# Experts of a routed MLP in seven groups of one, two or four, and conditioning sums by a ones column and two small DMAs

## The chip, the core and the metric

The kernel runs on one core of a Trainium2 chip. The metric is the device time of one launch in microseconds. The kernel before takes 1269.88 us, the median of three runs (1268.04 to 1272.34).

The engines are named as the profile names them: PE is TensorE (PEld its weight loads), DVE is VectorE, ACT is ScalarE, POOL is GpSimd, SP is SyncE. SP issues the weight loads here, POOL's queue the small transfers. PEclk is the granted clock of PE as a part of its full 2.4 GHz.

## The reference, cut to what matters

256 tokens of width 1024 pass through a first block with two layers and a second block with one. Each layer is modulated by a vector that comes from a condition `c`; the second block ends in 16 experts, of which each token uses two.

```python
def ada_modulation(c, w, b):                 # first block, 4 times; w is 1024 x 3072
    mod = jax.nn.silu(c) @ w + b
    shift, scale, gate = jnp.split(mod, 3, axis=-1)
    ...
h = x * (1.0 + scale) + shift
y = windowed_gqa(h, ...)                     # or recurrent_block(h, ...)
x = layer_norm(DN_ALPHA * x + (1.0 + gate) * y, ln_g[i, 0], ln_b[i, 0])
... the same again with sq_relu_mlp in the place of the mixer
mod_x = ada_modulation_2(cond_x, ada_w, ada_b)   # second block; w is 1024 x 6144
mod_c = ada_modulation_2(cond_c, ada_w, ada_b)

def moe_ffn(h, router_w, router_b, w_gate, w_up, w_down):
    probs = jax.nn.softmax(h @ router_w, axis=-1)
    ...  # best group of four experts by probs + router_b, then the two best experts in it
    for e in range(N_EXPERTS):               # 16 experts, 1024 -> 512 -> 1024
        he = (jax.nn.silu(h @ w_gate[e]) * (h @ w_up[e])) @ w_down[e]
        out = out + combine[:, e:e + 1] * he
```

Everything is in float32.

## The kernel before, in words

**Weights stream in.** A class `Stream` (`W`) holds one list of 1 MB weight loads in the order in which they are used. SP issues them (L193) into a ring of staging buffers `stg`: 5 of them, and for the experts 6 more, so that a load waits until PE has finished with the one 11 places before it. For dense layers ACT makes the high part `wh` of each weight (L218) and DVE the low part `wl` (L223), and each product is three matmuls (`mm3`, L380 to L382). Matmuls of the experts use the float32 weights directly.

**Conditioning runs as filler.** Weights of `ada_w` are spread among the items of the dense layers; `step` (from L229) takes one item at a time. Two ways are used. `ada_fill` multiplies on PE, four column groups of 32 at once (L424), and DVE copies the sums out as rows, `adaR` (L431). `ada_fill_v` accumulates on DVE (`adav`, L455 and L457), which leaves one partial sum on each partition. What is needed for shift and scale is 8 values on each of 128 partitions. Before, PE turns either form into that: `to_cols` (L500) by 16 matmuls for each row of `adaR`, with an identity's columns as the moving side, `sum_cols` (L472) by 8 matmuls for each vector with a column of ones. DVE then reads `gen`, the result in PSUM, and forms `sst` and `ab`, or `ss2`, from it (L559 to L567, L592 to L599). There are five such places: two layers of the first block by `to_cols`, one by `sum_cols`, and in the second block two rows by `to_cols` and one vector by `sum_cols`.

**After each dense layer** `post` runs `residual`: DVE multiplies by the gate, adds, and normalizes (`rr`, L865 to L867 and on), and PE waits for the normalized activations.

**The experts** (`moe_pass`). The router sorts the 14 experts behind the first two by their count of tokens; `RANK` says which place each gets. A selection matrix of ones and zeros (`Sg`) gathers the tokens of one window of 128 slots: `gather` makes the gathered activations by matmuls, `slots` the weights of each slot, `up` gate and up projections (L2406, activations stationary, 512 columns of the expert's weights moving) and the gated product, `turn` transposes it, `down` projects back (L2441), `scatter` adds the slots to their tokens (L2456, L2457). There are eight windows of two experts. In six of them each expert has 64 slots and its own half of PE's columns. In the two `SHARED` ones (1 and 3) two experts share the 128 slots, so each expert's weights pass over all 128 columns, as two separate units. The units are ten. Gate, up and down come as two loads each, so the 16 experts take 96 loads. The first two experts are fixed; the loads of the others wait until the routing is known. If the greatest count exceeds the slots, the whole runs again for the slots behind (`tc.If(over > CAP * base)`, up to three times).

Of the kernel before, what the change touches and what calls it, by code (L numbers as in the profile page):

```python
# [11 lines left out]
F32 = mybir.dt.float32  # L12
# [28 lines left out]
def _consts():  # L41
# [9 lines left out]
    small["slot"] = np.stack([p + 1 + CAP * i for i in range(4)], 1).astype(f)  # L51
# [83 lines left out]
class Stream:  # L135


    def __init__(self, tc, stage, parts, depth, ahead):
# [9 lines left out]
        self.more, self.since = None, 0  # L148

# [79 lines left out]
    def step(self, ahead=None):  # L229

        ahead = self.ahead if ahead is None else ahead
        i = self.pos
# [15 lines left out]
        return it[0], self.hl.pop(i)  # L248

# [21 lines left out]
def tile_model(ctx: ExitStack, tc: tile.TileContext, A, out):  # L271
# [6 lines left out]
    sml = ctx.enter_context(tc.tile_pool(name="sml", bufs=2))  # L278

# [270 lines left out]
    def ada1(i, j):  # L550
# [4 lines left out]
        def fin_ss(R, v=False):  # L555
            ab = cst.tile([128, 2, 8], F32, name=f"ab{idx}")
            tmp = sml.tile([128, 2, 8], F32, name="sst")
            pv = sum_cols(R, 2) if v else to_cols(R, 0)
            V.tensor_add(tmp[:, 0], pv[:, :, 0], adb[:, idx, 0])  # L559
            V.scalar_tensor_tensor(tmp[:, 1], pv[:, :, 1], 1.0, adb[:, idx, 1], op0=OP.add, op1=OP.add)  # L560
            if idx == 0:
                V.tensor_copy(ab[:, 0], tmp[:, 1])
                V.tensor_copy(ab[:, 1], tmp[:, 0])
            else:
# [3 lines left out]
            MOD[i, j] = ab  # L568
# [16 lines left out]
    def ada2(third):  # L585
# [3 lines left out]
        def fin(R):  # L589
            for row in range(2):  # L590
                pv = to_cols(R, row)
# [150 lines left out]
    def moe_items(add):  # L742
# [26 lines left out]
        for w in range(NWIN):  # L769
            for m in ((2 * w,), (2 * w + 1,)) if w in SHARED else ((2 * w, 2 * w + 1),):  # L770
                ups(m)
                if late is not None:
                    downs(late)
                    late = None
# [1519 lines left out]
    def moe_pass(base, W, weigh=None):  # L2294
# [166 lines left out]
        for u, (w, m) in enumerate(units):  # L2461
# [6 lines left out]
            if u:  # L2468
                turn(u - 1, mi())
# [92 lines left out]
```

## Time and profile before

| | us |
|---|---|
| median of three runs | 1269.88 |
| the profiled execution, its own time | 1271.62 |
| its span in the profile | 1269.8 |
| PE busy | 1209.9 (95%) |
| DVE busy | 779.3 (61%) |
| ACT busy | 557.8 (44%) |
| POOL busy | 96.3 (8%) |
| experts, first to last matmul of L2406 and L2441 | 988.4 to 1252.8 |

A busy share over the span is an average over stages. What bounds a stage is read in that stage: from the order of instructions on PE and the gaps between them, from the granted clock, and from which queue waits for which.

### The profile page before, as it was taken

Reading aid. Unit: us, or ns where it says so; the run is one execution under the profiler, and the core shown is the slowest. Engines: PE = TensorE matmul, PEld = TensorE weight load, DVE = VectorE, ACT = ScalarE, POOL = GpSimd, SP = SyncE. Lnnn points to the kernel's source line nnn. Section 1 sums busy time; section 2 is a strip of 40 time slices with the busy share of each in tenths; the row PEclk is TensorE's granted clock in tenths of the full one; section 3 lists DMA queues with packets and bytes.
Section 4 is the critical chain, followed back from the end, with each engine's and each line's share of the span. In section 5 each row is a group of like instructions: output and inputs, shape, how many; then the busy total and the mean of one; then the engine's idle time right before and its main releaser. Section 6 shows DMA issues by size and latency. Waiting matters only on the chain. (4 is left out here: it accounts for less than half of the span.)

```text
span 1269.8 us, 17771 instructions
## 1 busy us (share of the span) xinstructions
PE 1209.9 (95%) x6830; PEld 894.7 (70%) x6830; DVE 779.3 (61%) x1458; ACT 557.8 (44%) x944; POOL 96.3 (8%) x165
## 2 busy tenths in 40 slices
PE   5999799999989999979999999899998999999995
PEld 3757698999866668558989989899996444444432
DVE  3587879767575777685878759868898301110113
ACT  2455454534368766652455536634666111110111
POOL 6000360000013400010000000100000000000000
PEclk9999899989989999988999989999999899999997
DMA  9978498858684562487778846753338779889991
GB/s 291 343 306 301 167 324 318 302 198 305 192 250 123 178 200 69 165 292 253 268 257 288 297 135 201 231 168 117 127 106 324 282 289 413 327 346 375 409 412 53
DMA packets 146693, 317.52 MB, mean 250 GB/s; under 512 B 8120, under 2 KB 97368, under 8 KB 133288
## 3 DMA queue, kind: packets, MB, share of 16 engines
q1 hardware_dynamic: 139768, 304.17, 67.8%
q0 software_dynamic: 6832, 12.13, 3.1%
q8 instruction: 56, 0.92, 0.3%
q14 instruction: 37, 0.30, 0.1%
HBM read 315.23 MB, written 1.05 MB: 249 GB/s over the span
## 5 line engine op out<-in xcount | busy, mean ns | idle before, releaser
L218 ACT ACTIVATE wh<-stg 128x1024 fp32r<-128x1024 f32 x236 | 241.5, 1041 | 245.0 <-issue 98.1
L223 DVE TENSOR_TENSOR wl<-stg,wh 128x1024 fp32r<-128x1024 f32 x233 | 277.7, 1207 | 95.2 <-ACT wh L218 94.1
L380 PE MATMUL gen<-hH,wh 128*128 128x256 f32 x704 | 205.7, 292 | 3.7 <-ACT hH L841 2.6
L382 PE MATMUL gen<-hH,wl 128*128 128x256 f32 x704 | 203.8, 290 | 0.9 <-DVE wl L223 0.9
L381 PE MATMUL gen<-hL,wh 128*128 128x256 f32 x704 | 203.5, 290 | 0.5 <-DVE hL L845 0.5
L380 PEld LDWEIGHTS gen<-hH,wh 128*128 128x128 f32 x704 | 140.1, 199 | 10.4 <-ACT hH L841 4.6
L382 PEld LDWEIGHTS gen<-hH,wl 128*128 128x128 f32 x704 | 139.6, 199 | 2.4 <-DVE wl L223 2.3
L381 PEld LDWEIGHTS gen<-hL,wh 128*128 128x128 f32 x704 | 139.7, 199 | 2.0 <-POOL hL L845 0.7
L380 PE MATMUL acc<-wh,mH 128*128 128x512 f32 x256 | 102.0, 400 | 0.0
L381 PE MATMUL acc<-wl,mH 128*128 128x512 f32 x256 | 100.9, 394 | 0.0
L382 PE MATMUL acc<-wh,mL 128*128 128x512 f32 x256 | 100.7, 394 | 0.0
L2406 PE MATMUL mgu<-stg,wh 128*64 128x512 f32 (+1 forms) x256 | 83.7, 625 | 0.0
L457 DVE SCALAR_TENSOR_TENSOR adav<-stg,csil,adav 128x1024 f32<-128x1024 f32 (+2 forms) x56 | 79.2, 1415 | 6.7 <-DMA stg<-in_ada_w_dram 6.0
L2406 PE MATMUL mgu<-stg,wl 128*64 128x512 f32 (+1 forms) x256 | 78.5, 593 | 0.0
L2441 PE MATMUL mmi<-stg,mhT 128*64 128x512 f32 (+1 forms) x256 | 73.5, 595 | 0.0
L2412 DVE SCALAR_TENSOR_TENSOR mhid<-mgu,mws,mhid 128x512 f32<-128x512 f32 x10 | 7.5, 751 | 86.9 <-PE mgu L2406 86.9
L1492 PE MATMUL gen<-xr,bd 128*128 128x256 f32 (+1 forms) x224 | 59.6, 410 | 0.8 <-DVE xr L1468 0.8
L2441 PEld LDWEIGHTS mmi<-stg,mhT 128*64 128x64 f32 (+1 forms) x256 | 27.7, 150 | 42.3 <-issue 41.4
L2406 PEld LDWEIGHTS mgu<-stg,wl 128*64 128x64 f32 (+1 forms) x256 | 27.4, 150 | 42.7 <-issue 42.0
L2446 ACT ACTIVATE wh<-mmi 128x512 fp32r<-128x512 f32 x16 | 9.6, 597 | 108.5 <-PE mmi L2441 108.5
L380 PEld LDWEIGHTS acc<-wh,mH 128*128 128x128 f32 x256 | 48.8, 191 | 11.5 <-ACT wh L218 1.3
L382 PEld LDWEIGHTS acc<-wh,mL 128*128 128x128 f32 x256 | 48.6, 190 | 11.2 <-issue 0.8
(607 smaller groups left out, 2222.6 us busy)
## 6 DMA issues: line engine op xcount, KB each, us to landing
stg<-in_ada_w_dram SPq DMA_DIRECT2D x72, 1024.0 KB, 5.7
stg<-in_mlp_w_dram SPq DMA_DIRECT2D x64, 1024.0 KB, 5.8
stg<-in_moe_w_up_dram SPq DMA_DIRECT2D x32, 1024.0 KB, 8.6
stg<-in_moe_w_gate_dram SPq DMA_DIRECT2D x32, 1024.0 KB, 8.2
stg<-in_moe_w_down_dram SPq DMA_DIRECT2D x32, 1024.0 KB, 10.8
stg<-in_w_in_dram SPq DMA_DIRECT2D x20, 1024.0 KB, 5.4
stg<-in_rnn_w_in_dram SPq DMA_DIRECT2D x12, 1024.0 KB, 6.3
stg<-in_attn_w_in_dram SPq DMA_DIRECT2D x8, 768.0 KB, 9.2
```

The costliest lines, as they stand in the source:

```text
L218: nc.scalar.activation(h, t[:, sl], AF.Copy)
L223: sub()
L380: PE.matmul(o, ah, bh, start=first, stop=False)
L381: PE.matmul(o, ah, bl, start=False, stop=False)
L382: return PE.matmul(o, al, bh, start=False, stop=last)
L457: V.scalar_tensor_tensor(acc, tv[:, j, :], col[:, k:k + 1], acc, op0=OP.mult, op1=OP.add)
L1492: PE.matmul(pv[c0:c1, q, :], BD[g % 2][:, q, d, o:o + c1 - c0], xr[g][:, kt, :], start=(i == 0), stop=True, skip_group_check=True)
L2406: PE.matmul(ps[sl], gx[c][:, k, o + sl.start:o + sl.stop], t[:, 512 * k:512 * k + 512], start=first, stop=last)
L2412: V.scalar_tensor_tensor(hid, got[1], WS[w][:, j:j + 1], hid, op0=OP.mult, op1=OP.mult)
L2441: PE.matmul(ps[h][sl], hT[:, 2 * c + k, sl], t[:, 1024 * k + 512 * h:1024 * k + 512 * h + 512], start=begin and k == 0, stop=end and k == 1)
L2446: SC.activation(yH[:, h, :], ps[h], AF.Copy)
```

## The change

**Conditioning.** `to_cols` and `sum_cols` are gone. For the DVE form a new `sum_rows` multiplies with a column of ones that is broadcast over 32 columns, which leaves the sums as rows, two or four matmuls of 512 columns; ACT copies them to `adaR`. For both forms a new `row_cols` moves rows to columns by two DMAs on POOL's queue: the rows of `adaR` to a DRAM tile `flat`, and `flat` to `adaC`, 128 partitions of 8 or 16 values. The second waits for the first. The instructions of DVE that use `adaC` are put off by two steps of the stream (`LAG`, `wait_less`), or to the start of the next `post`, if that comes first.

**Experts.** The eight windows become seven, with 2, 1, 4, 2, 1, 2 and 4 experts of 128, 64 or 32 slots each, every expert on column groups of its own. There is no shared window, the units are seven, and the gathers are four groups instead of five. `RANK` puts the experts by their counts into these places. The loads of gate and up, and of down, go by half first and by expert second. The greatest count times the number of experts in its window decides whether a second pass runs.

```diff
-NWIN = 8
-SHARED = (1, 3)
-GROUPS = [(0,), (1, 2), (3, 4), (5, 6), (7,)]
-RANK = [0, 13, 2, 11, 1, 12, 3, 10, 4, 9, 5, 8, 6, 7]
+NUMBERS = [2, 1, 4, 2, 1, 2, 4]
+FIRST = [sum(NUMBERS[:w]) for w in range(len(NUMBERS) + 1)]
+NWIN = len(NUMBERS)
+GROUPS = [(0,), (1, 2), (3, 4), (5, 6)]
+RANK = [0, 6, 7, 8, 9, 2, 3, 1, 4, 5, 10, 11, 12, 13]
+LAG = 2
...
     def step(self, ahead=None):
         ahead = self.ahead if ahead is None else ahead
+        self.wait_less()
...
+    def wait_less(self, all=False):
+        for d in list(self.due):
+            d[0] -= 1
+            if all or d[0] < 0:
+                self.due.remove(d)
+                d[1]()
...
-    def sum_cols(acc, n):
-        ps = gen()
-        pv = ps[:, 0:8 * n].rearrange("p (k s) -> p k s", k=8)
-        for s in range(n):
-            for k in range(8):
-                PE.matmul(pv[:, k, s:s + 1], acc[:, 1024 * s + k:1024 * s + 1024:8], one, start=True, stop=True)
-        return pv
+    def sum_rows(acc, n):
+        ps = gen()
+        for g in range(2 * n):
+            PE.matmul(ps[32 * g:32 * g + 32, :], one.to_broadcast([128, 32]), acc[:, 512 * g:512 * g + 512],
+                      start=True, stop=True)
+        R = sml.tile([128, 512], F32, name="adaR", bufs=1)
+        SC.activation(R[:64 * n, :], ps[:64 * n, :], AF.Copy)
+        return R
+
+    def row_cols(R, row, n, use):
+        C = sml.tile([128, 2, 8], F32, name="adaC", bufs=3)
+        flat = rows.tile([2 * n, 512], F32, name="flat")
+        GP.dma_start(flat, R[row:64 * n:32, :])
+        GP.dma_start(C[:, :n, :], flat.rearrange("(s r) (p k) -> s (r p) k", s=n, k=8).rearrange("s p k -> p s k"))
+        W.due.append([LAG, lambda: use(C)])
...
-    def to_cols(R, row):
-        ps = gen()
-        pv = ps[:, 0:16].rearrange("p (k s) -> p k s", k=8)
-        for r in range(2):
-            for k in range(8):
-                PE.matmul(pv[64 * r:64 * r + 64, k, :], R[:, k::8], ident[:, 32 * r + row::64], start=True, stop=True)
-        return pv
...
-            pv = sum_cols(R, 2) if v else to_cols(R, 0)
-            V.tensor_add(tmp[:, 0], pv[:, :, 0], adb[:, idx, 0])
...
+            row_cols(sum_rows(R, 2) if v else R, 0, 2, use)
...
     def post(y, i, j, nxt):
+        W.wait_less(True)
...
-        def downs(w):
-            m = (2 * w, 2 * w + 1)
-            for i, h in ([(i, h) for i in m for h in range(2)] if w in SHARED else [(i, h) for h in range(2) for i in m]):
-                add(("moe_w_down_2", i, h), partial(down, i, h))
+        def downs(m):
+            for h in range(2):
+                for i in m:
+                    add(("moe_w_down_2", i, h), partial(down, i, h))
...
+        def lanes(w):
+            c = CAP // NUMBERS[w]
+            return [(FIRST[w] + n, slice(c * n, c * n + c)) for n in range(NUMBERS[w])]
...
-                        for j, t in enumerate(ts):
-                            sl = slice(0, 128) if len(m) == 1 else half[j]
+                        for (_, sl), t in zip(m, ts):
                             PE.matmul(ps[sl], gx[c][:, k, o + sl.start:o + sl.stop], t[:, 512 * k:512 * k + 512],
                                       start=first, stop=last)
```

What the change does to the order of instructions is shown at three places. The first is DVE around the first of the five conditioning results, in the attention layer: `den` and `sc` belong to its softmax, `wl` is the low part of a weight, `adav` the next vector's accumulation, `gate` the next gate. Before:

```order
L431 COPY adaR<-adaps 128x512
L1166 TENSOR_SCALAR sc<-sc,den 128x256 x4
L223 TENSOR_TENSOR wl<-stg,wh 128x1024
L457 SCALAR_TENSOR_TENSOR adav<-stg,csil,adav 128x1024
L559 TENSOR_TENSOR sst<-gen,adb 128x8
L560 SCALAR_TENSOR_TENSOR sst<-gen,adb 128x8
```

And DVE at the same place after:

```order
L442 COPY adaR<-adaps 128x512
L1176 TENSOR_SCALAR sc<-sc,den 128x256 x4
L224 TENSOR_TENSOR wl<-stg,wh 128x1024
L468 SCALAR_TENSOR_TENSOR adav<-stg,csil,adav 128x1024 x2
L224 TENSOR_TENSOR wl<-stg,wh 128x1024
L571 TENSOR_TENSOR sst<-adaC,adb 128x8
```

The first use stands behind one more accumulation and one more `wl`, and reads what a DMA brought instead of PSUM.

The second is DVE at the last of the five, in the second block's condition, at the start of `post`. Before:

```order
L485 SCALAR_TENSOR_TENSOR gate<-gen,gate 128x512
L599 TENSOR_TENSOR ss_132<-gen,adb_127 128x8
L865 TENSOR_TENSOR rr<-acc,gate 128x512
L866 TENSOR_TENSOR rr<-xnat,rr 128x512
L867 BN_STATS bst<-rr 128x6
L865 TENSOR_TENSOR rr<-acc,gate 128x512
```

After:

```order
L505 SCALAR_TENSOR_TENSOR gate<-gen,gate 128x512
L875 TENSOR_TENSOR rr<-acc,gate 128x512
L876 TENSOR_TENSOR rr<-xnat,rr 128x512
L877 BN_STATS bst<-rr 128x6
L610 TENSOR_TENSOR ss_134<-adaC,adb_129 128x8
L875 TENSOR_TENSOR rr<-acc,gate 128x512
```

The use has moved from ahead of the residual into it, behind its first half of a tile.

The third is PE among the experts. An instruction here stands for two records in the trace. Before, the first shared window (`mgu` gate and up, `mmi` the down projection and the transposes, `macc` the scatter):

```order
L2441 MATMUL mmi<-stg,mhT 64x512 x16
L2406 MATMUL mgu<-stg,wh 128x512 x4
L2406 MATMUL mgu<-stg,wl 128x512 x4
L2420 MATMUL mmi<-csm,mhid 128x128 x4
L2406 MATMUL mgu<-stg,wh 128x512 x4
L2406 MATMUL mgu<-stg,wl 128x512 x4
```

After, the last window, with four experts, from its gate and up to its scatter:

```order
L2395 MATMUL mgu<-stg,wl 32x512 x16
L2395 MATMUL mgu<-stg,wh 32x512 x16
L2395 MATMUL mgu<-stg,wl 32x512 x16
L2423 MATMUL mmi<-stg,mhT 64x512 x2
L2408 MATMUL mgu<-csm,mhid 128x128 x4
L2423 MATMUL mmi<-stg,mhT 64x512 x14
L2438 MATMUL macc<-wh,mst 128x512 x2
L2439 MATMUL macc<-wl,mst 128x512 x2
L2438 MATMUL macc<-wh,mst 128x512 x2
L2423 MATMUL mmi<-stg,mhT 32x512
L2439 MATMUL macc<-wl,mst 128x512 x2
L2423 MATMUL mmi<-stg,mhT 32x512 x31
```

Where four instructions of one expert went over 128 columns, sixteen of four experts now go over 32 columns each, and the last down projection waits for the loads of four experts.

## Rows read from the trace of the kernel before

**Rows 1.** The page's first part: busy time, share of the span, instructions.

```profile
PE   1209.9 (95%) x6830; PEld 894.7 (70%) x6830; DVE 779.3 (61%) x1458; ACT 557.8 (44%) x944; POOL 96.3 (8%) x165
```

**Rows 2.** Timeline of PE, the five blocks: start, us, engine, line, operation.

```profile
115.88 3.55 PE L500 MATMUL gen<-csm,adaR 128*64 128x2 f32 x32
...
274.95 7.54 PE L472 MATMUL gen<-csm,adav 128*128 128x1 f32 x32
...
589.38 6.48 PE L500 MATMUL gen<-csm,adaR 128*64 128x2 f32 x64
...
742.50 3.96 PE L472 MATMUL gen<-csm,adav 128*128 128x1 f32 x16
```

**Rows 3.** Stretches behind these blocks: us, busy by engine, PEclk, DMA share, GB/s.

```profile
120.20:123.80 3.60, 3.60 (x12) 2.83 (x11) 2.20 (x5) 1.89 (x3) 0.00 (x0) 0.53 1.10 350
...
282.40:287.60 5.20, 5.20 (x25) 5.20 (x26) 5.00 (x10) 0.00 (x0) 0.00 (x0) 0.50 0.19 63
...
488.90:492.40 3.50, 3.50 (x19) 3.50 (x18) 3.50 (x7) 0.00 (x0) 0.00 (x0) 0.51 0.00 0
...
595.80:601.70 5.90, 5.90 (x29) 5.90 (x29) 2.83 (x6) 0.00 (x0) 0.00 (x0) 0.51 0.26 87
...
746.40:751.80 5.40, 5.40 (x14) 4.24 (x14) 0.17 (x1) 0.00 (x0) 0.00 (x0) 0.50 0.50 172
```

**Rows 4.** Timeline of PE: a conditioning product in four column groups.

```profile
110.25 1.92 PE L424 MATMUL adaps<-stg,cS 128*32 128x512 f32 x16
```

**Rows 5.** DMA issues up to 960 us: queue, count, KB each, median us to landing.

```profile
bd<-in_rnn_w_a_dram POOLq DMA_DIRECT2D x8, 8.0 KB, 2.8
...
adb<-in_ada_b_dram POOLq DMA_DIRECT2D x4, 8.0 KB, 5.9
```

**Rows 6.** Timeline of POOL and DVE at the first and last block, idle before in brackets.

```profile
110.04 0.54 POOL L526 DMA_DIRECT2D lng<-in_ln_g_dram  x1 [83.68 <-DVE mx L1157]
...
113.06 0.66 DVE L431 COPY adaR<-adaps 128x512 f32<-128x512 f32 x1
...
753.26 0.69 DVE L865 TENSOR_TENSOR rr<-acc,gate 128x512 f32<-128x512 f32 x1 [6.59 <-PE acc L382]
```

**Rows 7.** Timeline of PE among the experts: pair, one expert, pair, shared window.

```profile
1027.07 7.09 PE L2441 MATMUL mmi<-stg,mhT 128*64 128x512 f32 x32
...
1041.50 3.60 PE L2406 MATMUL mgu<-stg,wh 128*128 128x512 f32 x8
...
1050.33 3.65 PE L2406 MATMUL mgu<-stg,wh 128*64 128x512 f32 x16
...
1070.62 14.00 PE L2441 MATMUL mmi<-stg,mhT 128*128 128x512 f32 x32
```

**Rows 8.** Stretches among the experts, columns as in group 3.

```profile
1034.00:1054.00 20.00, 20.00 (x64) 9.25 (x64) 1.44 (x2) 1.68 (x3) 0.00 (x0) 1.00 1.01 418
...
1154.00:1174.00 20.00, 20.00 (x81) 7.84 (x81) 1.69 (x4) 2.87 (x7) 0.00 (x0) 1.00 0.97 350
...
1214.00:1234.00 20.00, 20.00 (x93) 7.51 (x90) 1.69 (x4) 4.48 (x9) 0.00 (x0) 1.00 1.02 411
```

**Rows 9.** Waits of SP from 985 to 1255 us: us in total, times, longest.

```profile
SPq L193 <- PE mgu L2406: 153.7, 45, 16.7
```

**Rows 10.** Timeline of SP: start, us from first to last issue, queue, line, tile.

```profile
1011.43 16.07 SPq L193 DMA_DIRECT2D stg<-in_moe_w_up_dram  x2
```

**Rows 11.** DMA issues from 1027 to 1256 us, columns as in group 5.

```profile
stg<-in_moe_w_down_dram SPq DMA_DIRECT2D x28, 1024.0 KB, 10.9
stg<-in_moe_w_up_dram SPq DMA_DIRECT2D x25, 1024.0 KB, 8.5
stg<-in_moe_w_gate_dram SPq DMA_DIRECT2D x24, 1024.0 KB, 7.7
```

**Rows 12.** Timeline of PE: the end of the experts.

```profile
1245.70 7.09 PE L2441 MATMUL mmi<-stg,mhT 128*64 128x512 f32 x30
...
1254.22 0.72 PE L2457 MATMUL macc<-wl,mst 128*128 128x512 f32 x2
```

More of the change, by code (lines that the diff above doesn't have):

```diff
@@ L278, in tile_model @@
     sml = ctx.enter_context(tc.tile_pool(name="sml", bufs=2))
+    rows = ctx.enter_context(tc.tile_pool(name="rows", bufs=4, space=bass.MemoryType.DRAM))
     W = Stream(tc, stage, parts, NSTAGE, 1)
@@ L2332, in gather @@
                     s = Sg[:, t, j, :]
-                    for n, i in enumerate((2 * w, 2 * w + 1)):
+                    for i, sl in lanes(w):
                         p = pos0[:, t, i:i + 1] if i < 2 else pos1[:, t, i - 2:i - 1]
-                        if w not in SHARED:
-                            last = V.tensor_scalar(s[:, half[n]], iota[:, half[0]], p, None, op0=OP.is_equal)
-                        elif n == 0:
-                            last = V.tensor_scalar(s, iota, p, None, op0=OP.is_equal)
-                        else:
-                            last = V.scalar_tensor_tensor(s, iota, p, s.bitcast(F32), op0=OP.is_equal, op1=OP.add)
+                        last = V.tensor_scalar(s[:, sl], iota[:, 0:sl.stop - sl.start], p, None, op0=OP.is_equal)
             if g == 0 and weigh:
@@ L2422, in turn, with down @@
             SC.activation(hT, pv, AF.Copy)
[L2423 to L2425 removed]
+            HID[w] = hT
+        def down(w):
             ps = [mi() for _ in range(2)]
[L2428 to L2442 removed]
+            m = lanes(w)
+            hT = HID.pop(w)
+            for c in range(2):
+                ts = [W.take(("moe_w_down_2", i, c)) for i, _ in m]
+                for a, b in [(0, 0), (0, 1), (1, 0), (1, 1)]:
+                    k, h = (b, a) if c else (a, b)
+                    for (_, sl), t in zip(m, ts):
+                        PE.matmul(ps[h][sl], hT[:, 2 * c + k, sl], t[:, 1024 * k + 512 * h:1024 * k + 512 * h + 512],
+                                  start=c == 0 and k == 0, stop=c == 1 and k == 1)
             yH = parts.tile([128, 1024], F32R, name="wh").rearrange("p (h n) -> p h n", h=2)
@@ L2460, in moe_pass @@
         gather(0)
-        for u, (w, m) in enumerate(units):
-            rest = up(u)
-            if u == 0 and weigh:
+        for w in range(NWIN):
+            rest = up(w)
+            if w == 0 and weigh:
                 next(places[0])
-                own()
                 W.load_to(W.pos + W.depth)
             next(rest, None)
-            if u:
-                turn(u - 1, mi())
-            if m[0] == 2 * w:
-                slots(w)
-            if u == 0 and weigh:
+            if w:
+                turn(w - 1, mi())
+            slots(w)
+            if w == 0 and weigh:
                 next(places[0])
-            if m[-1] == 2 * w + 1 and w + 1 in starts:
-                if base and w == 0:
-                    own()
+            if w + 1 in starts:
                 gather(starts[w + 1])
             next(rest, None)
-            if u == 0 and weigh:
+            if w == 0 and weigh:
                 next(places[0], None)
-            for v in list(Y) if u < len(units) - 1 else ():
+            for v in list(Y) if w < NWIN - 1 else ():
                 scatter(v)
-            if u and units[u - 1][0] != w:
-                down(units[u - 1][0])
-        def between():
-            turn(len(units) - 1, pG.tile([128, 512], F32, name="mgu"))
-            for v in list(Y):
-                scatter(v)
-        down(NWIN - 1, between)
+            if w:
+                down(w - 1)
+        turn(NWIN - 1, pG.tile([128, 512], F32, name="mgu"))
+        for v in list(Y):
+            scatter(v)
+        down(NWIN - 1)
         scatter(NWIN - 1)
```

138 lines of the change are left out of this document (49 added, 89 removed).

## The prediction

> **What bounds the kernel now.** I read the page's first part, then PE's own timeline at the places the change touches, then tables by stretch, then who waits for whom. PE is busy 95% of the span [rows 1], so an instruction taken from PE is worth its time, unless something else is late in that stage. That has to be asked stage by stage. In the dense layers PE runs without gaps around the five conditioning blocks, and each block stands alone on it: PE does nothing but narrow matmuls there [rows 2]; four rows are shown, and the first stands for a like one at 484.87, too. Behind each of them the reader is to see a granted clock of 0.50 to 0.53, that is 1.2 GHz instead of 2.4, with PE still busy throughout [rows 3]. Among the experts PE is 100% busy too, and SP waits 153.7 us for PE's gate and up matmuls [rows 9]. So the staging ring is full there, the loads wait for PE, and PE sets the end. The DMA is not far behind, though: its share is 1.01 to 1.02 in the stretches where it runs freely, at 411 to 418 GB/s, and 0.97 with 350 in one where it does not [rows 8]. The two limits lie close together, and this decides the second part.
>
> The profiled execution took 1271.62 us, 1.7 more than the median of the runs. The sum is made against 1271.6; the forecast drops the difference again.
>
> **Part 1, conditioning: what goes.** The five blocks are 3.6, 7.5, 3.6, 6.5 and 4.0 us [rows 2], 25.2 us; ends overlap the next start by about 0.1 each, so they are worth 24.7. Nothing hides them: PE's next matmuls start as they end. With them, as I take it, goes the half clock behind them. At a granted clock c, a busy stretch of length t does the work of t·c, so it loses t·(1−c): 3.6·0.47 + 5.2·0.50 + 3.5·0.49 + 5.9·0.49 + 5.4·0.50 = 11.6 us [rows 3]. All five blocks show the same sequence, narrow matmuls of 1 or 2 columns and then the lower clock, while the 512-column matmuls ahead of them run at full clock. The unknown is whether another gap of PE brings the same drop back; the bounds are 0 and 11.6, and I take 11.6, since the cause in these rows is removed in all five places.
>
> **What comes.** `sum_rows` is four matmuls of 512 columns in four column groups, at one place, and two at another. The nearest row has eight such instructions (16 records) in 1.92 us [rows 4], so four cost 0.96, and two in two groups, side by side, the same: 1.9 in all. ACT's copies are two of some 0.6 us (DVE copies the same tile in 0.66 [rows 6]) on an engine busy 44% of the time: nothing. DVE's old work on `gen` becomes the same work on `adaC`: nothing.
>
> The DMAs are on POOL's queue. An issue from there lands in 2.8 us for one 8 KB pattern and 5.9 for another [rows 5], the second with the same 128 partitions of 2 by 8 values that `adaC` has. Two in a chain, with some half microsecond of issue each (0.54 for one from POOL [rows 6]), are 6.7 to 12.9 us, so `adaC` is there some 10 us after `adaR`. What POOL has queued behind the second's wait is, at the first place, loads of normalization constants (`lng`, `lnb`) that are wanted tens of microseconds later; PE and ACT wait for none of it. What DVE has queued behind its wait for `adaC` is what matters: low parts `wl`, without which PE's dense matmuls stop.
>
> At each place I compare the time at which `adaC` lands with the time at which DVE gets to it. First: the copy ends at 113.7 [rows 6], the values land at 120.4 to 126.6, and DVE, behind one more `adav` and one more `wl`, gets there at about 123: a stall of 0 to 3.6, taken as 1. Second: about 11 us of `wl`, `adav` and MLP work stand between; 0 to 1.5, taken as 0. Third: two `wl` and some small work, 0 to 5, taken as 1. Fourth: two `wl` and two `adav`, 0 to 4, taken as 2 (the second row's use lands next to the first's). Fifth: `post` forces the use, in the middle of the residual chain that PE waits for. That chain began at 753.26, as soon as PE was through [rows 6]; PE now gets there 4.0 − 1.0 + 2.7 = 5.7 earlier, at 747.6, DVE does half a tile in 2.1 and stands at 749.7, while the values come at 751 to 757: 1 to 7.5, taken as 4. Together 8 us of a possible 0 to 21.
>
> Conditioning: −24.7 + 1.9 − 11.6 + 8 = **−26 us**. The bounds are −24.7 + 1.9 − 11.6 = −34 with no stall, and −24.7 + 1.9 + 21 = −2 with every stall and no clock back.
>
> **Part 2, the experts.** Instruction by instruction on PE: two experts on halves of the columns take the time of one (3.65 us for 16 records against 3.60 for 8 [rows 7]), since the halves run side by side. A unit is four such rows for gate and up, 13.7 us net of overlap, and 6.9 for down (7.09 for a pair, 14.00 for a shared window of two [rows 7]): 20.6 us. Ten units become seven, so 3 × 20.6 = 61.8 us of PE go, if four experts on quarters also take the time of one. The trace has that form: 16 records in four groups took 1.92 us, four rounds of 0.48 [rows 4], against 0.45 for a record alone [rows 7]. I take it as free.
>
> The Trainium skill speaks against this a little (TensorE: Matmul & The Clock Gate, section "Measured speedup vs the span model"): three column tiles gave 2.38 times the throughput, not 3. By that a unit of four experts would be some 26% longer, an estimate of 5 us for each of the two. This case's row agrees better with no loss (4 × 0.45/0.48 = 3.75 times).
>
> PE alone would end at 1254.9 − 61.8 = 1193, with 1254.9 the end of the last scatter [rows 12]. But then the loads are late. The 96 loads of 1.0486 MB stay. Of them 77 are issued from 1027 on [rows 10, 11], when the routing is known, and the change moves neither the routing nor what is loaded ahead of it. At 415 GB/s, the rate of the stretches in which the DMA ran freely [rows 8], a load takes 2.53 us and 77 take 195, so the last lands at 1027.2 + 195 + 2 = 1224. Behind it stand a last half of four down projections, 3.5 us at full clock or 6.9 at half (PE will have waited for loads by then; I keep both levels as bounds and take the lower), and the eviction and scatter, about 2.2 us from the last down matmul to the end as now [rows 12]: PE ends at about **1231**, between 1225 and 1241. The epilogue of some 15 us behind it stays. So the experts give 1254.9 − 1231 = **24 us** (14 to 30) of the 62 that PE loses; the rest goes into waits for loads.
>
> **Sum.** 1271.6 − 26 − 24 = 1221.6, and 1.7 less against the median: **1220 us**. If both parts do their worst inside their bounds, −2 − 14 gives 1254; at their best, −34 − 30, it is 1206.
>
> **The rivals.**
>
> *A. The forecast*, 1220, chance 0.62.
>
> *B. The DMA hops cost what PE saved.* For it: both hops are serial, the use is only two steps later, and behind each DVE wait stand the `wl` that PE needs; and the clock may drop again where PE then waits. Against it: at four of five places DVE has 3 to 11 us of other work in between. With conditioning at −3 and the experts at −24 it gives 1243. Chance 0.17. The Trainium skill (DMA: Bandwidth & Descriptors, section "Anatomy of one DMA — SWDGE (gpsimd) path") puts about 2 us of fixed cost on each such DMA and most of it on confirming the write, worst where the target is HBM, which `flat` is; by its figure two hops would be 4 us, an estimate, under the rows' 5.6 to 11.8. No row of the trace writes to DRAM from this queue.
>
> *C. The DMA does not hold 415 GB/s for 195 us.* For it: one stretch of the middle stands at 350 with a share of 0.97, hardly idle [rows 8]. Against it: SP was waiting for PE in that part [rows 9], and where it was not, 411 and 418 held for 20 us at a time. At 350 a load takes 3.0 us, 77 take 231, PE ends at 1267 instead of 1254.9, and 1271.6 − 26 + 12 − 2 = 1256. Chance 0.12. The Trainium skill (Perfetto Trace Analysis, section "Roofline") gives 358 GB/s for a core whose neighbour shares the memory and about 435 for one alone; by 358 the time would be some 1251, an estimate; the row at 418 agrees with the second.
>
> *D. The counts overflow, and the experts run twice.* This is the one on the other side. A window of four has 32 slots for each expert instead of 64. Worked out from the reference's inputs, the experts there have at most 28 tokens, those in the windows of two at most 60 of 64. From the 33rd token on, the whole repeats: 96 more loads at 2.53 us are 243, and the time is some 1460. Chance 0.02.
>
> *E. Four column groups do not run at once,* for four different expert weights, so the change does not do what it says. Then a window of four takes 82 us instead of 20.6. Two of them add 123 to PE's 1193, the loads no longer matter, PE ends at 1316, and 1271.6 − 26 + 61 − 2 gives 1305, slower. The point from which PE decides again is 1231, or 19 us more in each of the two. The four-group row speaks against it [rows 4]; its stationary side is shared, which theirs is not. Chance 0.03.
>
> The last 0.04 is for a mishap that leaves the time about as it was.
>
> **How the numbers follow.** The likeliest is A, 1220. The range takes A's bound of 1206 at the bottom, where PE has no stall, and reaches over B to 1250 at the top; C, D and E lie outside with 0.17, the mishap with 0.04. About 0.3% (4 us) is what a measurement of this kernel can tell from no change. A, B and C are faster by more, 0.91; D and E slower, 0.05, and a little more of the last case, 0.06; the same is 0.03.
>
> **What would show it.** Right: none of the narrow rows on PE; a granted clock near 1.0 where group 3 has 0.5; among the experts about 20.6 us of matmuls for seven units; SP's waits for PE gone down from 153.7 us, and in their place PE's waits for DMA of some 35 us; a DMA share of 1.0 from 1000 us on to the end, at 410 or more. Part 1 is wrong if DVE shows waits of over 3 us for `adaC` at more than two places, or if PEclk stays at 0.5 behind them. Part 2 is wrong if the four-expert units take more than 20.6 us without waiting, or the DMA share falls below 0.95 while SP is not waiting.

## The result and the profile after

The changed kernel takes 1219.7 us, the median of four runs (1217.34 to 1222.46), against 1271.1 of the kernel before on the same chip. The ratio is 0.960, with a 95% interval from 0.957 to 0.963: 51 us less. The forecast was 1220.

The page of the kernel after, its first part (busy time, share of the span, instructions) and three rows of its second part (tenths busy of PE, the granted clock and the DMA share, in 40 slices of the span, some 30 us each):

```profile
PE 1128.1 (93%) x6610; PEld 822.0 (67%) x6610; DVE 771.6 (63%) x1448; ACT 552.4 (45%) x935; POOL 104.2 (9%) x177
...
PE   5999699999989999979999999899999997989884
...
PEclk9999889999999999989999999999999899999998
DMA  9988498988694572478779766653346769999993
```

PE has 82 us less work than in [rows 1], but the span is only 52 shorter: PE now waits in places. Most of them are at the end, among the experts, where the DMA row stands at 9 from some 1000 us on.

**Conditioning.** The narrow blocks of [rows 2] are gone. Behind the places where they stood, the stretches that answer to [rows 3] (us, then busy time of PE, PEld, DVE, ACT, POOL, the granted clock, the DMA share and GB/s):

```profile
125.40:131.00 5.60, 4.67 (x11) 3.77 (x12) 3.64 (x10) 0.86 (x2) 0.34 (x1) 0.50 0.91 337
277.00:283.00 6.00, 6.00 (x44) 5.55 (x43) 5.89 (x6) 2.61 (x3) 0.76 (x1) 1.00 0.79 239
474.00:480.00 6.00, 4.81 (x42) 4.61 (x41) 6.00 (x10) 4.32 (x7) 0.00 (x0) 1.00 0.01 3
575.00:582.00 7.00, 7.00 (x41) 6.10 (x40) 2.86 (x3) 2.61 (x3) 1.49 (x2) 1.00 0.98 346
722.00:727.00 5.00, 5.00 (x23) 4.12 (x22) 3.75 (x7) 0.00 (x0) 1.60 (x3) 1.00 0.83 284
```

At four places the clock stays at full. At the first it falls to 0.50 again, and PE has idled there. The timelines of DVE and PE at that place say why (start, us, engine, line, operation, and in brackets the idle time before with what ended it):

```profile
119.32 1.22 DVE L224 TENSOR_TENSOR wl<-stg,wh 128x1024 fp32r<-128x1024 f32 x1 [1.15 <-ACT wh L219]
125.42 0.17 DVE L571 TENSOR_TENSOR sst<-adaC,adb 128x8 f32<-128x8 f32 x1 [4.88 <-DMA adaC<-flat]
125.51 0.16 DVE L572 SCALAR_TENSOR_TENSOR sst<-adaC,adb 128x8 f32<-128x8 f32 x1
125.58 0.69 DVE L505 SCALAR_TENSOR_TENSOR gate<-gen,gate 128x512 f32<-128x512 f32 x1
```

```profile
120.92 1.89 PE L1192 MATMUL gen<-PT,vN 128*128 128x256 f32 x8
126.33 3.78 PE L1192 MATMUL gen<-PT,vN 128*128 128x256 f32 x8 [3.52 <-DVE gate L505]
```

DVE stands 4.88 us for the second DMA. The `gate` behind it empties a PSUM buffer that PE needs, so PE stands 3.52 us, and its next matmuls run at half clock. Where the first place had cost PE 3.6 us of narrow matmuls, it now costs a wait of about the same length, and the half clock came back with it. DVE's other waits for `adaC` are 3.08 us at the third place and 4.96 at the fourth; at the second and fifth it had none.

**Experts.** Stretches, with the columns as above, and the waits of PE and of its weight loads for the DMA (us in total, times, longest; the two overlap):

```profile
990.00:1000.00 10.00, 10.00 (x33) 4.32 (x33) 0.91 (x2) 1.43 (x4) 0.00 (x0) 1.00 0.11 20
...
1160.00:1180.00 20.00, 16.57 (x75) 4.98 (x70) 1.44 (x2) 1.77 (x3) 0.00 (x0) 1.00 1.02 410
```

```profile
PEld mgu L2395 <- DMA stg<-in_moe_w_up_dram: 22.0, 11, 3.1
PE mgu L2395 <- DMA stg<-in_moe_w_up_dram: 13.0, 9, 2.1
PE mmi L2423 <- DMA stg<-in_moe_w_down_dram: 3.8, 6, 0.7
PEld mmi L2423 <- DMA stg<-in_moe_w_down_dram: 10.1, 9, 1.6
```

and one step of four experts on quarters of the columns, which answers to [rows 7]:

```profile
1005.02 3.64 PE L2395 MATMUL mgu<-stg,wh 128*32 128x512 f32 x32
```

Thirty-two records in 3.64 us, as long as sixteen for a pair: the quarters run at once, with four different stationary sides. From the first expert matmul to the last scatter it is 243.8 us (959.5 to 1203.3), against 266.6 before. PE has stopped setting the end; it waits for loads, at 410 to 420 GB/s.

### The profile page after: what moved, and what is told of

Read it like the earlier page. It is cut to its first block, busy times and chain, and to the rows that moved or that the text cites. A ratio compares the mean times of both kernels' runs of the same rounds, so it can differ in the third digit from the quotient of the medians.

```text
span 1218.2 us, 17320 instructions
## 1 busy us (share of the span) xinstructions
PE 1128.1 (93%) x6610; PEld 822.0 (67%) x6610; DVE 771.6 (63%) x1448; ACT 552.4 (45%) x935; POOL 104.2 (9%) x177
## 5 line engine op out<-in xcount | busy, mean ns | idle before, releaser
L391 PE MATMUL gen<-hH,wh 128*128 128x256 f32 x704 | 198.5, 282 | 4.3 <-ACT hH L851 3.0
L393 PE MATMUL gen<-hH,wl 128*128 128x256 f32 x704 | 197.2, 281 | 5.0 <-DVE wl L224 5.0
L392 PE MATMUL gen<-hL,wh 128*128 128x256 f32 x704 | 196.3, 279 | 1.3 <-DVE hL L855 1.3
L391 PEld LDWEIGHTS gen<-hH,wh 128*128 128x128 f32 x704 | 133.7, 190 | 12.1 <-ACT hH L851 5.7
L392 PEld LDWEIGHTS gen<-hL,wh 128*128 128x128 f32 x704 | 133.5, 190 | 3.2 <-POOL zp L1458 1.1
L2423 PE MATMUL mmi<-stg,mhT 128*32 128x512 f32 (+2 forms) x256 | 69.6, 599 | 7.7 <-SPq L2486 3.9
L2395 PE MATMUL mgu<-stg,wh 128*32 128x512 f32 (+2 forms) x256 | 66.6, 648 | 5.9 <-DMA stg<-in_moe_w_up_dram 5.9
L2395 PE MATMUL mgu<-stg,wl 128*32 128x512 f32 (+2 forms) x256 | 65.1, 595 | 7.2 <-DMA stg<-in_moe_w_up_dram 7.2
L2423 PEld LDWEIGHTS mmi<-stg,mhT 128*32 128x32 f32 (+2 forms) x256 | 20.2, 129 | 54.5 <-issue 36.2
L2429 DVE TENSOR_TENSOR wl<-mmi,wh 128x512 fp32r<-128x512 f32 x14 | 9.7, 692 | 74.0 <-ACT wh L2428 74.0
## 6 DMA issues: line engine op xcount, KB each, us to landing
stg<-in_attn_w_in_dram SPq DMA_DIRECT2D x8, 768.0 KB, 10.4
```

The costliest lines, as they stand in the source:

```text
L391: PE.matmul(o, ah, bh, start=first, stop=False)
L392: PE.matmul(o, ah, bl, start=False, stop=False)
L393: return PE.matmul(o, al, bh, start=False, stop=last)
L2395: PE.matmul(ps[sl], gx[c][:, k, o + sl.start:o + sl.stop], t[:, 512 * k:512 * k + 512], start=first, stop=last)
L2423: PE.matmul(ps[h][sl], hT[:, 2 * c + k, sl], t[:, 1024 * k + 512 * h:1024 * k + 512 * h + 512], start=c == 0 and k == 0, stop=c == 1 and k ...
L2429: V.tensor_sub(yL[:, h, :], ps[h], yH[:, h, :].bitcast(F32))
```

## The experiments

All medians are of four runs (six for the last), each beside runs of the kernel before on the same chip, which stood at 1270 to 1271.

| kernel | median, us | ratio to before, 95% interval |
|---|---|---|
| changed kernel | 1219.7 | 0.957 to 0.963 |
| conditioning alone | 1239.8 | 0.973 to 0.979 |
| experts alone | 1251.6 | 0.983 to 0.988 |
| LAG = 6 | 1213.7 | 0.952 to 0.960 |
| windows 2, 4, 1, 2, 1, 2, 4 | 1205.7 | 0.943 to 0.952 |
| uses ordered behind a low part | 1210.3 | 0.950 to 0.955 |
| the last two together | 1198.5 | 0.942 to 0.949 |
| narrow blocks, contiguous | 1220.7 | 0.960 to 0.963 |
| wide blocks | 1224.2 | 0.963 to 0.966 |
| narrow blocks as before | 1232.5 | 0.968 to 0.971 |
| 16 loads less, on the changed kernel | 1198.2 | 0.938 to 0.944 |
| 16 loads less, on the kernel before | 1262.8 | 0.991 to 0.996 |
| kernel before with a pad | 1259.6 | 0.988 to 0.994 |

The dense matmuls (`mm3`) are the same 4176 records in all these kernels, in the same order but for some 80, so two traces can be set against each other record by record (this is called the alignment below). The table says by how many us a kernel's trace is ahead of the kernel before at the same matmul; times are those of the kernel before. The kernel with the experts alone, whose conditioning is that of before, stands 0.5 to 3.1 us ahead at these places, so a difference of up to some 3 us says nothing.

| at, us | where | changed | conditioning alone | blocks as before | uses ordered | pad |
|---|---|---|---|---|---|---|
| 104 | ahead of the first place | 0.3 | -0.2 | 1.8 | -0.9 | 0.0 |
| 158 | behind it | -1.3 | 0.0 | 2.1 | 4.3 | 0.0 |
| 271 | ahead of the second | 1.2 | 2.1 | 4.5 | 6.1 | 2.6 |
| 290 | behind it | 10.1 | 10.9 | 5.2 | 15.0 | 3.0 |
| 470 | ahead of the third | 13.4 | 11.9 | 7.9 | 17.4 | 5.2 |
| 520 | behind it | 16.1 | 14.4 | 7.1 | 19.9 | 4.5 |
| 560 | ahead of the fourth | 16.0 | 13.4 | 6.2 | 19.0 | 3.6 |
| 640 | behind it | 25.0 | 23.1 | 8.3 | 29.8 | 6.3 |
| 700 | ahead of the fifth | 24.0 | 22.5 | 9.5 | 30.5 | 7.2 |
| 755 | behind it | 30.1 | 28.8 | 9.7 | 36.6 | 9.2 |
| 960 | ahead of the experts | 30.6 | 31.4 | 9.3 | 37.2 | 13.6 |

**Each part alone.** The first kernel has the diff's conditioning part alone, the second the rest alone.

> The kernel before with the conditioning part alone (row sums, two DMAs, uses put off); the experts stay in eight windows. The forecast's sum gives -26 us against the kernel before for this part. Aligned matmul by matmul, the traces of before and after stand 30.5 us apart at the last router product, so this kernel should be 30 us faster than before, 1240. If the two parts act on each other (earlier arrival at the experts costs something there), it is nearer 26, 1244. If the gain before the experts came from elsewhere, it is under 15.

> The kernel before with the expert part alone (seven windows of 2, 1, 4, 2, 1, 2, 4 experts); conditioning by narrow matmuls as before. The forecast gives -24 us. From the traces, 51.6 us of span less 30.5 leave 21: expected 21 to 24 faster than before, 1247 to 1250. The rival that the loads cannot hold their rate over the whole stretch would show under 10.

Conditioning alone gains 30.4 us, the experts alone 18.6, together 49.0 of the 51.4 of both. Within the spread of the runs the parts do not act on each other: aligned among the experts, the trace of conditioning alone is 30.2 us ahead at 1000 and 30.2 at 1247. The experts alone gained 2 us less than the bottom of the expected range; the interval, 15 to 22 us, reaches into it.

**A longer lag.**

```diff
-LAG = 2
+LAG = 6
```

> The changed kernel with LAG = 6 instead of 2: DVE's use of the DMA's values is put off by six steps of the stream. Theory: DVE's waits for the DMA (4.9 us at the first place, 5.0 at the fourth) go, and with the first also PE's wait of 3.5 us for the gate behind it and the half clock after that; 5 to 9 us faster than the changed kernel, 1211 to 1215. Rival: the waits were covered by low parts made ahead, and nothing moves: 1219.

The median fell by 6, but the intervals overlap, and DVE's waits are still there. On its timeline:

```profile
118.87 1.23 DVE L224 TENSOR_TENSOR wl<-stg,wh 128x1024 fp32r<-128x1024 f32 x1 [0.99 <-ACT wh L219]
124.57 0.17 DVE L571 TENSOR_TENSOR sst<-adaC,adb 128x8 f32<-128x8 f32 x1 [4.47 <-DMA adaC<-flat]
```

`sst` still stands behind the same `wl`. The code asks for it later, yet on the engine it stands where it stood. So this run did not test the theory. The next one keeps `LAG = 6` and orders each use behind the newest low part that had been given out when the lag ran out:

```diff
-                            sub()
+                            self.low = sub().ins
...
-                d[1]()
+                with self.tc.issue_after(self.low):
+                    d[1]()
```

> As the run with LAG = 6, but each use of the DMA's values is also ordered behind the newest low part (wl) that DVE had been given when the lag ran out. With LAG alone the order on DVE at the first and fourth place had stayed as it was (use behind one wl there, waits of 4.5 and 5.0 us), so that run tested nothing. Theory: both waits go; at the first place PE's wait of 3.5 us for the gate behind it and the half clock after it go too, about 5 us; at the fourth PE loses little today. 4 to 8 us less than the changed kernel: 1212 to 1216. Rival: waits of DVE cost nothing and the median of 1214 with LAG alone was the spread of runs: 1217 to 1222.

1210.3, or 9.4 us under the changed kernel. On its timeline PE no longer waits for `gate` at the first place:

```profile
120.30 1.88 PE L506 MATMUL gen<-adav,csm 128*128 128x512 f32 x4
122.01 3.62 PE L1194 MATMUL gen<-PT,vN 128*128 128x256 f32 x16
```

The alignment puts the gain where the waits were: from a loss of 1.6 us over the first place (0.3 to -1.3) to a gain of 5.2 (-0.9 to 4.3), and from 9.0 to 10.8 over the fourth, which is no more than the scatter. DVE's waits for `adaC` are 1.8 us in all. The wait at the first place does cost, and the lag alone does not set the order.

**What sets the end among the experts.** One of SP's two long waits in the changed kernel lies early among the experts, from 982 to 998 us (waits from 975 to 1000 us; the other, of 17.4 us, ends at 967):

```profile
SPq L194 <- PE mgu L2395: 24.1, 3, 14.8
```

The ring is full there: the second window has one expert, whose six loads PE takes 20 us to work off, and the DMA stands at 20 GB/s from 990 to 1000 us. So a kernel with the four-expert window second:

```diff
-NUMBERS = [2, 1, 4, 2, 1, 2, 4]
+NUMBERS = [2, 4, 1, 2, 1, 2, 4]
...
-RANK = [0, 6, 7, 8, 9, 2, 3, 1, 4, 5, 10, 11, 12, 13]
+RANK = [6, 7, 8, 9, 0, 2, 3, 1, 4, 5, 10, 11, 12, 13]
...
+            if w == 0:
+                gather(starts[1])
+                turn(0, mi())
...
-            if w:
-                down(w - 1)
+            if w != 1:
+                down(max(w - 1, 0))
```

> The changed kernel with windows of 2, 4, 1, 2, 1, 2, 4 experts, the first window's down projection taken ahead of the second window, and the ranks moved accordingly. In the changed kernel SP waits 14.8 us for PE early among the experts (982 to 998 us), the ring being full of one slow single-expert window's loads, and the DMA moves 20 GB/s from 990 to 1000. Theory: the experts end with their loads, so filling that hole brings up to 14 us: 1205 to 1212. Rival: the end is set by PE or by the last window, and nothing or a loss of a few us comes (1217 to 1225).

1205.7, a gain of 14 by the medians, with runs from 1198.9 to 1211.4. The same ten microseconds of the DMA now:

```profile
990.00:1000.00 10.00, 10.00 (x58) 3.30 (x58) 1.85 (x6) 1.51 (x6) 0.00 (x0) 1.00 1.01 419
```

First matmul to last scatter are 233.4 us instead of 243.8, so 10.4 us of the gain lie in the experts. SP's other long wait, up to 967 us, is still there, with 17.9 us. The other test takes loads away. Each expert's second half of the down weights is not loaded, and the first half is used twice:

```diff
-            for h in range(2):
-                for i in m:
-                    add(("moe_w_down_2", i, h), partial(down, i, h))
+            for i in m:
+                add(("moe_w_down_2", i, 0), partial(down, i, 0))
```

> The changed kernel without the second half of each down projection's weights: 16 of the 96 loads are left out, and the first half's weights are used for both halves, so the matmuls are as many. Theory: the experts end with their loads; 16 loads of 2.53 us less are 40 us, until PE sets the end: 25 to 35 us faster than the changed kernel, 1185 to 1195, and PE's waits for loads all but gone. Rival: the end is set by PE or the windows' chains: 1217 to 1222.

> The kernel before with the same 16 loads left out. Theory: PE sets the end there, the loads waited for it; 0 to 3 us faster, 1267 to 1271. Rival: the loads set the end in both kernels, and it gains 20 us or more.

The changed kernel gains 21.5 us, with 217.9 us from first matmul to last scatter; the kernel before gains 7. So the loads set the end in the changed kernel, and mostly not before. Both came out off the expected size. Without the 16 loads the changed kernel's DMA runs dry before PE does: from 1130 on it falls below its rate, and PE is left with the last window's work.

```profile
1130.00:1150.00 20.00, 16.71 (x113) 5.38 (x110) 1.30 (x5) 3.64 (x10) 0.00 (x0) 0.95 0.90 348
1150.00:1170.00 20.00, 19.02 (x74) 6.02 (x74) 2.13 (x3) 1.79 (x3) 0.00 (x0) 0.88 0.84 337
1170.00:1180.00 10.00, 9.54 (x71) 3.52 (x70) 2.76 (x5) 1.28 (x3) 0.00 (x0) 1.00 0.00 0
```

Why the kernel before gains as much as 7 with PE busy all the time stays open: it is even until 1155 and ahead only in the last windows, where the instructions of the two halves stand in another order.

**What the narrow blocks were worth.** Two kernels put blocks of constants back on PE where rows are sent, one with 2 moving columns, one with 256:

```diff
+        ps = gen()
+        pv = ps[:, 0:16].rearrange("p (k s) -> p k s", k=8)
+        for r in range(2):
+            for k in range(8):
+                PE.matmul(pv[64 * r:64 * r + 64, k, :], ident[:, 8 * k:8 * k + 64], ident[:, 32 * r::64], ...)
```

```diff
+        ps = gen()
+        for k in range(8):
+            PE.matmul(ps[:, 0:256], ident, cS.rearrange("p k n -> p (k n)"), start=True, stop=True)
```

> The changed kernel with 16 narrow matmuls (64 columns stationary, 2 moving) of constants put on PE at each of the six calls that send a row through the DMAs; their result is not read. Each block takes 3.5 us, six take 21. Theory: a half clock of some 3 to 6 us of work follows each of the five places, as in the kernel before, so 21 + 10 = 31 us slower than the changed kernel: 1248 to 1254, granted clock 0.5 behind the blocks. Rival: the half clock has nothing to do with these blocks: 21 slower, 1241.

> The same with 8 matmuls of 256 moving columns and 128 stationary at each of the six calls, of about the same 3.4 us each; their result is not read. Theory: the clock stays at 1.0 behind them, and only their own time is added: 20.5 us, 1238 to 1242. Rival: any added block brings the drop: as with the narrow ones.

Both theories missed. The narrow blocks take half of what `to_cols` took, 1.8 us instead of 3.5, since their stationary side is read in one piece: a weight load takes 138 ns, where one at a stride of 8 elements takes 217. Behind them the clock stays at full, and the kernel is 1 us slower. The wide ones put 21 us on PE and cost 4.5. At the first place they cost nothing: PE would have waited, and with work in the gap its clock stays at 1.00:

```profile
114.00:118.00 4.00, 4.00 (x21) 3.45 (x20) 3.96 (x4) 1.10 (x2) 0.04 (x1) 1.00 1.06 373
118.00:124.00 6.00, 6.00 (x28) 4.47 (x27) 0.62 (x6) 2.14 (x3) 1.24 (x2) 1.00 1.07 375
```

Neither is a copy of what was removed. The third comes near: 64 columns read at a stride of 8 elements, 16 or 32 instructions at the same five places, results unused. (At the second and fifth place those removed had 128 stationary columns and 1 moving, 7.54 and 3.96 us; the copies take 6.48 and 3.55. The block of constants `csm` is widened to 512 columns for this run.)

```diff
+    def cols_again():
+        ps = gen()
+        pv = ps[:, 0:16].rearrange("p (k s) -> p k s", k=8)
+        for r in range(2):
+            for k in range(8):
+                PE.matmul(pv[64 * r:64 * r + 64, k, :], csm[:, k:512:8], ident[:, 32 * r::64], start=True, stop=True)
```

> The changed kernel with narrow matmuls put back on PE as they stood before: 64 stationary columns read at a stride of 8 elements, 2 moving, of constants, 16 instructions (3.5 us) at the first, third and fifth place and 32 (7.1 us) at the second and fourth; results are not read. The blocks of the earlier run had contiguous columns and took only 1.8 us each, and the clock stayed at 1.00 behind them, so they were no copy. Theory: 25 us of PE and 6 to 12 us of half clock come back, less some 5 at the first place, where PE waits anyway: 24 to 32 us slower than the changed kernel, 1244 to 1252, with granted clocks near 0.5 behind the blocks. Rival: PE has slack there (the wide blocks cost 4 us for 21 us of matmuls): 5 to 8 us slower, 1226.

1232.5, 12.8 us over the changed kernel: between both. The half clock is back behind the blocks (stretches with a block, and behind it):

```profile
477.00:480.50 3.50, 3.50 (x34) 3.47 (x33) 2.30 (x3) 3.43 (x4) 0.00 (x0) 0.84 0.00 0
480.50:485.00 4.50, 4.50 (x22) 4.50 (x22) 4.50 (x8) 0.00 (x0) 0.00 (x0) 0.50 0.00 0
...
732.50:736.30 3.80, 3.80 (x36) 3.34 (x32) 2.42 (x4) 1.11 (x2) 0.57 (x1) 0.88 0.31 82
736.30:741.00 4.70, 4.70 (x13) 3.72 (x14) 0.00 (x0) 0.00 (x0) 1.60 (x3) 0.50 0.76 249
```

By the alignment the blocks cost 21.3 us up to the experts (30.6 against 9.3). Of these, 4.7 came back around the router and the first gather, 940 to 971 us, and 2.8 later, in a run whose loads came at 420 to 424 GB/s where the changed kernel had 412 to 421. Around the router it is the clock: the changed kernel had 0.73 and 0.76 from 950 to 960 and from 960 to 970 us, which loses 5.1 us, and this run 1.00 from 952 to 982. Whether that hangs on the blocks is not shown, and why the rate differs between runs stays open.

**The rest.** With the blocks back, 9.3 us of gain are still there: 1.8 ahead of the first place, and the rest growing slowly, most of it away from the five places. It is in the 256-column matmuls of the MLPs. The same line, first of before and then of after (operation, tiles, count: shortest, median and longest in ns, first and last start, shape):

```profile
L380 PE MATMUL gen<-hH,wh x704: 277/283/681, 150.9 to 740.4; 128*128 128x256 f32 x176
```

```profile
L391 PE MATMUL gen<-hH,wh x704: 276/276/682, 152.0 to 715.5; 128*128 128x256 f32 x176
```

In steady stretches of the MLPs (160 to 270, 300 to 345 and 645 to 735 us) they follow each other at 120 ns before and with the experts alone, at 114 to 116 in every kernel with the new conditioning. The change adds one tile, `adaC`, to the pool `sml`, and so moves whatever is placed in SBUF behind it. The last run gives the kernel before a tile of that size, used once at the start, and nothing else:

```diff
+    nc.vector.memset(sml.tile([128, 2, 8], F32, name="pad", bufs=3), 0.0)
```

> The kernel before with one more small tile, three buffers of 64 bytes on each partition, in the pool in which the change puts adaC, and one memset of it at the start; all other instructions stand in the same order. In all kernels with the changed conditioning, also in the one with narrow blocks put back, the 256-column matmuls of the MLPs (gen) follow each other at 114 ns, against 120 in the kernel before and in the one with the expert part alone; over some 2,000 of them that is some 10 us, about the 9.3 us by which the kernel with the narrow blocks put back is still ahead of the kernel before at the experts. Theory: what moved is the place of tiles in SBUF behind that pool; with the pad alone the cadence goes to 114 ns and the kernel is 8 to 11 us faster than before, 1259 to 1262. Rival: the cadence hangs on the removed waits or on the DMAs, and the pad changes nothing: 120 ns, 1268 to 1272.

1259.6, or 10.7 us faster (by the interval, 8 to 15), in the expected range, and its row reads as that of after:

```profile
L382 PE MATMUL gen<-hH,wh x704: 276/276/682, 150.9 to 732.1; 128*128 128x256 f32 x176
```

**A version faster than both.** Both findings together, the windows 2, 4, 1, 2, 1, 2, 4 and the uses ordered behind a low part:

> The window order 2, 4, 1, 2, 1, 2, 4 and the uses ordered behind the newest low part, together. If the one acts before the experts and the other in them, the gains add: 1219.7 - 14 - 5 = 1200 to 1203. If the loads reach the experts no earlier for PE's earlier arrival, only the larger stands: 1206.

1198.5, under the expected range: 72 us less than the kernel before and 21 less than the changed one. Its alignment ahead of the experts is 40.9 us, and the experts take 233.0.

## Why the prediction held, term by term

The total was right, 1220 against 1219.7. That it came so close is luck: one term had been left out, and others were off the other way by as much.

| term of the sum | forecast, us | measured, us | from |
|---|---|---|---|
| narrow blocks and half clock behind them | -36.3 | -33 | blocks put back, stretch by stretch: their own 23.6, and some 9.6 of half clock |
| `sum_rows` | +1.9 | +2.1 | the two blocks of line 481, 1.06 and 1.05 us |
| DVE's waits for the DMAs | +8 | +6.6 to +9.4 | uses ordered: by the alignment, by the medians |
| place of tiles in SBUF | not named | -9 | left with the blocks put back; the pad: -11 |
| conditioning | -26 | -30.4 | that part alone |
| experts | -24 | -18.6 to -21 | alone, and in the trace |

The rows of the conditioning part add up to -31 to -34, and the part measured -30.4. The -33 is a sum of stretches and no difference of times: put back, the blocks cost 21.3 us by the alignment, since they also fill waits of PE.

*The blocks and the clock.* The step held. The clock is at full behind four of five places, as said, and it falls to 0.50 again when the blocks are put back. All the traces say the same: of the five kernels with such blocks (before, experts alone, 16 loads less on the kernel before, pad, blocks as before) each has a stretch at 0.50 behind each of the last four places, and of the nine others none has one there. With the block's length, and the clock behind it as in the rows above, the second place is worth 8.2 us and the fifth 6.2; the alignment gives 8.2 and 6.0. (The differences of "changed" and "blocks as before" over a place.)

*The waits.* At three places the alignment falls short of such a sum: the first is worth 4.4 us (a block of 3.5, and 0.9 of clock) and gave -1.9, the third 5.75 and gave 3.5, the fourth 8.8 and gave 6.9. That is 6.3, 2.3 and 1.9 us, some 10 together, the last two within the scatter, and not all of it is the DMAs. At the first place PE stands 3.52 us, and the ordered run gains 6.8 us there. At the third, DVE's wait for `adaC` ends at 455.9 us and PE has no gap near it. PE's gap comes later, for a low part that stands behind the recurrent block's scans on DVE, and the ordered run has the same gap of 1.19 us:

```profile
479.78 0.38 PE L393 MATMUL gen<-hH,wl 128*128 128x256 f32 x1 [1.19 <-DVE wl L224]
```

At the fourth PE's one gap is 0.43 us. So the DMAs cost what the ordered run gave back, 6.6 to 9.4 us against 8, and nearly all of it at the first place. The size was near, the places were not. The prediction had named a sign against its first part, and it came: DVE waits more than 3 us for `adaC` at three places (4.88, 3.08 and 4.96), where more than two were to speak against it, and behind the first the clock is at 0.50. The first was taken as 1 us and cost all that the change had saved there: the values were used 12.0 us after their copy had ended (113.47 to 125.42), near the late end of the range, and I had looked only at `wl` behind DVE's wait. What hurt was `gate`, because it frees a PSUM buffer; the half clock behind PE's wait came on top. The fifth was taken as 4 and cost nothing, since ACT's copy came early enough. The issues of the two hops in the changed kernel's trace (count, KB, median us to landing):

```profile
flat<-adaR POOLq DMA_DIRECT2D x5, 8.0 KB, 3.7
adaC<-flat POOLq DMA_DIRECT2D x5, 8.0 KB, 5.5
```

The Trainium skill (DMA: Bandwidth & Descriptors, "Anatomy of one DMA — SWDGE (gpsimd) path") gives some 2 us of fixed cost for a DMA from that queue. The trace agrees where the DMA engines stood idle: 1.7 us for the first hop at the second place (share 0.02) and 2.2 for the second at the third (0.05). Where they were busy with other loads the hops are longer, 5.6 and 5.7 us at the first place (shares of 1.02 and 1.05).

*The term not named.* The sum took it that nothing else of the conditioning part touches PE. No row of before could have told that a tile of 192 bytes per partition would make other matmuls 5% faster; but a pool that grows in a diff moves tiles, and that could have been named as an unknown of either sign. Without it the conditioning part would have come out at -21, and the forecast 9 us too low. The better place came by accident.

*The experts.* The forecast had 242.6 us from first matmul to last scatter; it was 243.8. Its sum had slipped: 1224, 6.9 for the last half at the lower clock and 2.2 for the eviction and scatter make 1233, not 1231, so the term should have read 22. Either lies about 1 us from the measured length, for the tail itself was sized too long: the clock stayed at 1.00 there, and the last scatter ended some 6 us behind the last load. That PE's 62 us would give way to a bound by loads, and give 24, is what the two runs with less loads and the run with the other window order show. One sentence in it was wrong: the loads do not stop until 1027 because the routing isn't known. They stop because the ring is full, SP waiting for PE's gate and up matmuls, before (14.9 us at that place) as after; otherwise the other window order could not have gained 10.4 us there. The forecast's time did not hang on it, since the change leaves that stop where it was (998.1 us, 38.6 behind the first expert matmul, as it was 38.8 before). Some 2 us of the term were lost ahead of it, where the routing's matmuls ran at a lower clock (0.73 from 950 to 960 us, against 0.97 from 976 to 988 before). Of the signs named for this part, SP's waits for PE's gate and up matmuls fell only from 153.7 to 101.9 us, and PE's own waits for loads are 16.8 us (32.1 on its weight loads) where some 35 were named; the rate and the share of the DMA are as forecast.

*The rivals.* B, hops that eat the gain, was right for the first place alone. C is refuted: the loads held 410 to 421 GB/s for 180 us. That speaks for the second of the two figures in the Trainium skill (Perfetto Trace Analysis, "Roofline"), some 435 for a core alone, and not for 358. D and E did not occur; four quarters take 3.64 us where two halves take 3.65.

## What to carry to other kernels

When a long wait is moved to another engine's queue, look at everything behind it there, and first at what frees a buffer of the engine that bounds the stage. An order in the code is not an order on the engine: look it up, and tie the late use to an instruction if it has to stay late. When PE stops being the bound of a stage that streams weights, ask next where the loads stand still: here one slow window early in the stage held the ring full, and moving it was worth more than half as much as the expert change itself. A wait in an engine's row is not yet a cost: of three waits of DVE of 3 to 5 us here, only one made PE stand for more than half a microsecond.

## What the runs showed of the hardware that had not been expected

- A tile of 192 bytes on each partition, placed ahead of others in SBUF, brought the 256-column matmuls of the MLPs from 120 to 114 ns apart and the kernel before from 1270.3 to 1259.6 us, with all other instructions in the same order. Which tile's place it is, and what about it, was not tried.
- A weight load of 64 columns read at a stride of 8 elements made a narrow matmul last 111 ns from start to start (16 instructions, 32 records, in 3.55 us); of contiguous columns, half of that.
- Blocks of the first kind, 32 records in 3.5 us, left the clock at 0.50 behind them. Of the second kind, 64 records in 3.3 us at the fourth place, they left it at 1.00. Work put into a gap of PE kept the clock at 1.00 where the gap alone had left it at 0.50.
